# The state-space units of a hybrid decoder block, run in a staggered order of groups and chunks

## The chip, the core and the metric

The kernel runs on one core of one Trainium2 chip. The metric is the device time of one execution in microseconds (us); a smaller time is better. Three executions took 1394.72, 1395.9 and 1400.18 us, so the median is 1395.9 us.

## What is computed

One decoder block over 512 tokens of width 1024 in float32: a normalisation, one wide input projection, three token mixers in parallel (an attention with selected keys, an attention with compressed, selected and windowed keys, and a state-space mixer), gates that merge the three, an output projection, and a feed-forward part. The change touches the order of work in the state-space mixer, which the reference writes as

```python
cb = jnp.einsum('bcign,bcjgn->bcijg', cm, bm)
y_diag = jnp.einsum('bcijg,bcijgh,bcjgh,bcjghp->bcighp', cb, lmat, dtc, xs)
states = jnp.einsum('bcjgn,bcjgh,bcjghp->bcghpn', bm, decay_states * dtc, xs)
def step(h, inp):
    s_c, d_c = inp
    return h * d_c[..., None, None] + s_c, h
_, h_in = lax.scan(step, h0, (jnp.moveaxis(states, 1, 0), jnp.moveaxis(chunk_decay, 1, 0)))
y_off = jnp.einsum('bcign,bcghpn,bcigh->bcighp', cm, h_in, jnp.exp(a_cum))
y = y_diag + y_off + xs * d_skip.reshape(SSD_GROUPS, SSD_HPG)[:, :, None]
```

There are 4 groups (g) of 8 heads and 4 chunks (c) of 128 tokens. Chunk c of a group needs the state that chunk c-1 of the same group leaves behind; different groups do not depend on each other.

## The kernel before

Two generators write the program. `main` holds the latency-bound work: the index of the first attention, its units, then `ssd`, then the units of the second attention. `filler` holds the large projections: in this order z0 to z3, x0 to x3 (the inputs of the state-space groups 0 to 3), nq (the queries of the second attention), the merge gates, the branch products. `main` yields an amount of time after each piece, and the loop at the end lets `filler` emit that much; where `main` yields a name, such as `x2`, `filler` runs on until that part is emitted. The instructions of `main` get a higher priority (`HI`, `HM`), and the scheduler of the framework then lays out each engine's order, so that projection matmuls fill the places where `main` waits. PE, ACT, DVE and POOL each work through their own order, and SP issues nearly all DMAs in its order.

`ssd` runs 16 units, one for each (group, chunk). A unit goes through three parts.

- `stage1` takes a tile `bcx` (three matrices of the chunk) and a tile `E`, and has SP load both (L1248, L1250). `load_xz` loads `xz`, the inputs and the gate values (L1257). `xz` has two buffers, `bcx` and `E` have three.
- `stage2`: a small matmul (L1264), POOL masks `E` (L1265), ACT takes eight exponentials (L1268), POOL scales `xz` into `xt` (L1270), into `xw` where there is a next chunk (L1273), and by the skip weights (L1277). DVE multiplies `E` (L1275).
- `stage3`: where there is a chunk before, PE multiplies its state `hst` (L1286), DVE and POOL finish that (L1288, L1289). Where there is a chunk after, PE makes the new state (L1293), and ACT copies it (L1296) or POOL and DVE add it to the old one (L1298, L1299). Eight matmuls of `xt` with `E` follow (L1303, two passes each), DVE adds and gates the result (L1307, L1308), and ACT squares it into the gate half of `xz` (L1309). After that square the buffer of `xz` is free, and `load_xz` of the unit after the next is emitted. Four transposes (L1314) and a store end the unit one step later.

The list `order` sets which (group, chunk) is the unit number 0 to 15; `need(i)` yields `x` and `z` of a group before its chunk 0. Projection matmuls stand on L451 to L453, the transposes of the x projection on L835, those of nq on L601, the splitting of weights on L170 and L172, the convolution of x on L821 to L828.

Of the kernel before, what the change touches and what calls it, by code (L numbers as in the profile page):

```python
# [40 lines left out]
def build_kernel(ctx, tc, A, out):  # L41
# [1195 lines left out]
    def ssd(sv, ratio):  # L1237
# [82 lines left out]
            yield ratio * 100  # L1320

        TR = []
        order = [(g + i, c) for g in (0, 2) for c in range(4) for i in range(2)]

        def need(i):
            if i < 16:
# [341 lines left out]
    def main():  # L1668
        nonlocal at
        HI[0] = 0  # L1670
        yield from dsa_index(mk)
        yield "dq"
        yield "nkv"
        sv, *rest = yield from ssd_prelude()
        at = popen("att", side="right")
        HI[0] = HM
        us = dsa_units()
        us[5].load = lambda: ssd_prelude2(sv, *rest)
        us[7].load = lambda: ssd_prelude3(sv, rest[0])
        yield from pipeline(us, R1)  # L1680
        pclose("att")
        pclose("pre")
        pclose("mask")
        yield from ssd(sv, R3)
        XT[0] = "pT"
        yield "nq"
        at = popen("att", side="right")
        yield from pipeline(nsa_units(R2), R2)
        done.add("nsa")
        yield "c1"  # L1690
        pclose("att")
        pclose("kv")
# [60 lines left out]
```

## Time and profile before

| what | value |
|---|---|
| median of three executions | 1395.9 us |
| lowest and highest | 1394.72 and 1400.18 us |
| the profiled execution's own time | 1403.27 us |
| its span, first to last instruction | 1401.5 us |
| mean granted clock of TensorE, as a share of full speed | 0.986 |

The profile is one execution, about 7 us above the median. Its sums are made against its own span. A row of a timeline has a start, a duration, the engine, the line, the operation and its tiles, and in brackets the idle time of the engine before it with what ended that. `PEld` is the load of a matmul's weights, which overlaps `PE`.

### The profile page before, as it was taken

The page shows a single profiled execution, that of the slowest core. Times are in us where ns is not written, and L with a number is a line of the kernel's source. Part 1 is how long each engine was busy: PE and PEld are TensorE (multiplying, and loading weights), DVE is VectorE, ACT ScalarE, POOL GpSimd, SP SyncE. Part 2 cuts the span into 40 slices and gives each one's busy share as a digit, 9 for nine tenths or more (in the row PEclk, how much of TensorE's full clock was granted, in tenths as well). Part 3 has the DMA queues.
Part 4 walks back from the last instruction along what each step waited for, and adds up shares of the span by engine and source line. Part 5 has one row for each costly group of instructions (what it writes and reads, how often), then busy time and mean ns, then how long its engine had stood idle before and what let it go on. Part 6 is the DMA issues. An engine that isn't in the chain of part 4 may idle for free.

```text
span 1401.5 us, 19674 instructions
## 1 busy us (share of the span) xinstructions
PE 1369.0 (98%) x6875; PEld 1142.1 (81%) x6875; DVE 1001.1 (71%) x1962; ACT 722.0 (52%) x1434; POOL 286.8 (20%) x235
## 2 busy tenths in 40 slices
PE   8989999999999999999999999999899999999998
PEld 7878888888877778888887888788789888888887
DVE  6499977999877656477667788888635575767841
ACT  5545436667666756366565566555224444444430
POOL 3445211111047375100000002133100201102000
PEclk9999999999999999999999999999999999999999
DMA  6335654644486687735435453435444665746531
GB/s 192 89 96 144 166 179 132 166 113 123 121 259 223 190 257 201 188 100 140 114 114 157 118 146 111 122 117 177 143 150 140 118 177 127 174 116 132 157 117 52
DMA packets 222721, 205.35 MB, mean 147 GB/s; under 512 B 15497, under 2 KB 170013, under 8 KB 222622
## 3 DMA queue, kind: packets, MB, share of 16 engines
q1 hardware_dynamic: 206652, 180.49, 43.7%
q0 software_dynamic: 15232, 20.98, 8.2%
q10 hardware_dynamic: 738, 2.63, 0.6%
q8 instruction: 54, 0.88, 0.3%
q14 instruction: 45, 0.37, 0.1%
HBM read 167.56 MB, written 36.51 MB: 146 GB/s over the span
## 4 chain that ended last, share of the span: by engine, by line
PE 77%; DVE 7%; DMA 7%; issue 4%; POOL 3%; ACT 2%; SPq 0%; DVEq 0%; POOLq 0%; ACTq 0%
PE pj L451 18%; PE pj L453 18%; PE pj L452 18%; PE sc L451 3%; PE sc L452 3%; PE sc L453 3%; DMA gld<-g_d 3%; PE pT L931 2%; PE sc L893 2%; PE sc L892 2%; PE pv L944 2%; DMA wraw<-in_w_in_dram 1%; PE pv L943 1%; POOL mixf L1488 1%; PE sc L1303 1%
## 5 line engine op out<-in xcount | busy, mean ns | idle before, releaser
L170 ACT ACTIVATE whi<-wraw 128x1024 fp32r<-128x1024 f32 (+2 forms) x190 | 198.3, 1048 | 233.8 <-PE pj L452 115.7
L172 DVE TENSOR_TENSOR wlo<-wraw,whi 128x1024 fp32r<-128x1024 f32 (+1 forms) x169 | 215.7, 1280 | 104.5 <-ACT whi L170 102.9
L451 PE MATMUL pj<-hTh,whi 128*128 128x512 f32 x384 | 153.6, 400 | 0.2 <-DVE cacc L824 0.2
L453 PE MATMUL pj<-hTh,wlo 128*128 128x512 f32 x384 | 152.6, 397 | 0.0
L452 PE MATMUL pj<-hTl,whi 128*128 128x512 f32 x384 | 152.3, 397 | 0.0
L451 PE MATMUL pj<-whi,hTh 128*128 128x512 f32 (+2 forms) x352 | 138.7, 394 | 5.9 <-DVE stk L521 3.2
L901 ACT ACTIVATE p<-p,nb,rs 128x256 f32<-128x256 f32 (+3 forms) x192 | 123.2, 645 | 30.6 <-DVE nb L899 30.6
L453 PE MATMUL pj<-whi,hTl 128*128 128x512 f32 (+2 forms) x352 | 137.8, 392 | 0.1
L452 PE MATMUL pj<-wlo,hTh 128*128 128x512 f32 (+2 forms) x352 | 137.6, 391 | 0.0
L451 PE MATMUL pj<-yh,whi 128*128 128x512 f32 (+1 forms) x288 | 109.7, 387 | 11.0 <-DVE gld L1485 6.4
L452 PE MATMUL pj<-yl,whi 128*128 128x512 f32 (+1 forms) x288 | 109.2, 379 | 0.0
L453 PE MATMUL pj<-yh,wlo 128*128 128x512 f32 (+1 forms) x288 | 108.9, 378 | 0.0
L452 PE MATMUL pj<-h2l,whi 128*128 128x512 f32 (+1 forms) x256 | 96.3, 376 | 0.0
L453 PE MATMUL pj<-h2h,wlo 128*128 128x512 f32 (+1 forms) x256 | 96.2, 376 | 0.0
L451 PE MATMUL pj<-h2h,whi 128*128 128x512 f32 (+1 forms) x256 | 96.1, 376 | 0.0
L987 POOL DMA_DIRECT2D qu<-q_d x32 | 23.5, 735 | 334.9 <-PE sc L893 259.3
L451 PEld LDWEIGHTS pj<-hTh,whi 128*128 128x128 f32 x384 | 72.4, 189 | 14.0 <-DVE cacc L824 0.4
L452 PEld LDWEIGHTS pj<-hTl,whi 128*128 128x128 f32 x384 | 72.4, 189 | 13.8 <-issue 0.5
L453 PEld LDWEIGHTS pj<-hTh,wlo 128*128 128x128 f32 x384 | 72.4, 189 | 13.8 <-issue 0.2
L451 PEld LDWEIGHTS pj<-whi,hTh 128*128 128x128 f32 x352 | 67.4, 192 | 19.8 <-issue 5.8
L935 ACT ACTIVATE pth<-pT 128x512 fp32r<-128x512 f32 x95 | 54.5, 592 | 47.4 <-PE pT L931 46.9
L453 PEld LDWEIGHTS pj<-whi,hTl 128*128 128x128 f32 x352 | 67.4, 191 | 12.4 <-DVE hTl L427 0.4
(385 smaller groups left out, 3294.9 us busy)
## 6 DMA issues: line engine op xcount, KB each, us to landing
wraw<-in_w_in_dram SPq DMA_DIRECT2D x84, 512.0 KB, 4.7
wraw<-in_w_ff_dram SPq DMA_DIRECT2D x58, 512.0 KB, 4.3
qd<-in_w_ff_dram POOLq DMA_DIRECT2D x18, 512.0 KB, 6.0
q_d<-qev SPq DMA_DIRECT2D x64, 128.0 KB, 2.5
qu<-q_d POOLq DMA_DIRECT2D x32, 256.0 KB, 3.7
E<-ac_d SPq DMA_DIRECT2D x16, 512.0 KB, 4.9
xz<-xz_d SPq DMA_DIRECT2D x16, 512.0 KB, 5.8
gld<-g_d SPq DMA_DIRECT2D x32, 256.0 KB, 2.8
```

What stands on the lines that cost most here:

```text
L170: act.activation(hi[:, :m], r[:, :m], AF.Copy)
L172: (pool if i in LOWP else dve).tensor_tensor(lo[:, :m], r[:, :m], f(hi[:, :m]), op=ALU.subtract)
L451: pe.matmul(o, lh, rh, start=first, stop=False)
L452: pe.matmul(o, lh, rl, start=False, stop=False)
L453: pe.matmul(o, ll, rh, start=False, stop=last)
L892: pe.matmul(s_[:, h % w, :n], u.q[h], kh[:, :n], start=True, stop=False)
L893: pe.matmul(s_[:, h % w, :n], u.q[h], kl[:, :n], start=False, stop=True)
L901: act.activation(u.p[h][:, :n], u.p[h][:, :n], AF.Exp, bias=u.nb[:, h:h + 1], scale=rs8[:, u.b, u.h0 + h:u.h0 + h + 1], accum_out=u.sm[:, ...
L931: pe.transpose(pt[:, h], u.p[h][:, kb * 128:kb * 128 + 128], ident)
L935: act.activation(ph, ptf, AF.Copy)
L944: pe.matmul(o, vk, pl0, start=False, stop=en)
L987: pool.dma_start(q.rearrange("p (i a) c -> p i (a c)", i=2), src)
```

## The change

The list `order` is written out. Before, two groups alternate through all four chunks: (0,0) (1,0) (0,1) (1,1) and so on to (1,3), then the same with groups 2 and 3. Now group 0 runs its first two chunks, and each later group joins in one or two places behind: its first unit stands between units of the group before. Number, size and content of the units are the same.

```diff
-        order = [(g + i, c) for g in (0, 2) for c in range(4) for i in range(2)]
+        order = [(0, 0), (0, 1), (1, 0), (0, 2), (1, 1), (0, 3), (1, 2), (2, 0), (1, 3), (2, 1), (3, 0), (2, 2), (3, 1), (2, 3), (3, 2), (3, 3)]
```

In what follows u0 to u15 are the places in `order`. The orders below are those of PE and POOL; a line of three dots stands for projection matmuls (L451 to L453).

PE from the end of u0's matmuls to the first of u2, before (u1 is (1,0), u2 is (0,1); `xt` is the scaled input, `hst` a state, `craw` the x projection after its convolution):

```order
L1303 MATMUL sc<-xt,E 128x64 x6
L835 MATMUL pF<-ident,craw 128x128 x4
...
L1264 MATMUL pv<-bcx 128x128
L1303 MATMUL sc<-xt,E 128x64 x5
L1314 MATMUL pT<-ident,yv 128x128
L1293 MATMUL pT<-xw,bcx 128x512
L1314 MATMUL pT<-ident,yv 128x128 x3
L1303 MATMUL sc<-xt,E 128x64 x3
L1286 MATMUL sc<-hst,bcx 128x512
...
L1303 MATMUL sc<-xt,E 128x64 x3
```

The same stretch of PE now (u1 is (0,1), u2 is (1,0)):

```order
L1303 MATMUL sc<-xt,E 128x64 x6
L835 MATMUL pF<-ident,craw 128x128 x4
L1286 MATMUL sc<-hst,bcx 128x512
...
L1264 MATMUL pv<-bcx 128x128
...
L1303 MATMUL sc<-xt,E 128x64 x3
L1314 MATMUL pT<-ident,yv 128x128 x4
L1293 MATMUL pT<-xw,bcx 128x512
L1303 MATMUL sc<-xt,E 128x64 x5
...
L1303 MATMUL sc<-xt,E 128x64 x8
```

The product with the state moves ahead, since u1 now needs u0's state, and u2's matmuls stand behind 24 projection matmuls where there were 33.

PE around the last transposes of the x projection, before (the first L1303 row is u8, the last is u9, group 3's first unit):

```order
L1303 MATMUL sc<-xt,E 128x64 x5
L1264 MATMUL pv<-bcx 128x128
L835 MATMUL pF<-ident,craw 128x128 x4
...
L835 MATMUL pF<-ident,craw 128x128 x4
...
L1264 MATMUL pv<-bcx 128x128
L1314 MATMUL pT<-ident,yv 128x128 x4
...
L601 MATMUL pF<-ident,qraw 128x128 x4
...
L1303 MATMUL sc<-xt,E 128x64 x3
```

PE there now, from the end of u7 to the start of u9, which is (2,1); u10 is group 3's first unit:

```order
L1303 MATMUL sc<-xt,E 128x64 x5
L1264 MATMUL pv<-bcx 128x128
L1286 MATMUL sc<-hst,bcx 128x512
L835 MATMUL pF<-ident,craw 128x128 x4
...
L1303 MATMUL sc<-xt,E 128x64 x5
L1314 MATMUL pT<-ident,yv 128x128 x4
L1303 MATMUL sc<-xt,E 128x64 x3
L1286 MATMUL sc<-hst,bcx 128x512
L1264 MATMUL pv<-bcx 128x128
L835 MATMUL pF<-ident,craw 128x128 x4
...
L1303 MATMUL sc<-xt,E 128x64 x3
```

Before, the last four transposes were followed by 47 projection matmuls and nothing of u9; now they are followed by 13 and then by u9, which does not need group 3.

POOL, the piece of the difference at u2 and u3 (`E` is the decay matrix that POOL masks):

```order
 L1265 AFFINE_SELECT E<-E 128x1024
 L1277 TENSOR_TENSOR xz<-xz,dskip 128x512
+L1298 TENSOR_TENSOR hst<-hst,sv_dec 128x512
+L1289 TENSOR_TENSOR t_4105<-t_4105,xz 128x512
 L1265 AFFINE_SELECT E<-E 128x1024
-L1298 TENSOR_TENSOR hst<-hst,sv_dec 128x512
+L1270 TENSOR_TENSOR xt<-xz,sv_dth 128x512
+L1273 TENSOR_TENSOR xw<-xz,sv_dw 128x512
+L1277 TENSOR_TENSOR xz<-xz,dskip 128x512
+L1265 AFFINE_SELECT E<-E 128x1024 x2
 L1270 TENSOR_TENSOR xt<-xz,sv_dth 128x512
```

The masks of two later units (`x2`) now stand ahead of the scaling of u3's `xz`.

## Rows read from the trace of the kernel before

**Rows 1.** The page: the span, and each engine's busy time, share of the span and instructions.
```profile
span 1401.5 us, 19674 instructions
PE 1369.0 (98%) x6875; PEld 1142.1 (81%) x6875; DVE 1001.1 (71%) x1962; ACT 722.0 (52%) x1434; POOL 286.8 (20%) x235
```

**Rows 2.** Waits of PE, whole span: who waited for whom; us in total, times, longest.
```profile
PE sc L1303 <- POOL xt L1270: 6.3, 4, 2.2
PE pT L1293 <- POOL xw L1273: 0.7, 1, 0.7
PE pj L451 <- ACT yh L807: 4.6, 2, 2.7
PE pj L451 <- DVE gld L1485: 6.4, 8, 1.9
```

**Rows 3.** Where the projection stands: first and last of its steps, and unit 0's first load.
```profile
351.54 0.76 ACT L821 ACTIVATE cacc<-pj,convc 128x512 f32<-128x512 f32 x1
L835 PE MATMUL pF<-ident,craw x80: 270/272/300, 273.0 to 482.6; 128*128 128x128 f32 x80
390.61 0.38 SPq L1248 DMA_DIRECT2D bcx<-bct_d  x1
```

**Rows 4.** Chain of waits, 396 to 444: start us, us, what; two starts of projection matmuls included.
```profile
...
397.06 0.24 PE pj L451
...
401.16 0.23 PE pj L451
401.38 0.86 PE pT L1293 x2
...
403.09 0.28 PE pv L1264 x2
403.37 1.29 PE sc L1303 x12
404.66 0.44 PE pF L835 x4
...
442.20 0.91 PE sc L1286 x2
...
```

**Rows 5.** From unit 0's gate to unit 2's scale: timelines of ACT, SP and POOL.
```profile
410.60 0.62 ACT L1309 ACTIVATE xz<-yv 128x512 f32<-128x512 f32 x1
411.34 0.36 SPq L1257 DMA_DIRECT2D xz<-xz_d  x1
417.57 1.04 POOL L1270 TENSOR_TENSOR xt<-xz,sv_dth 128x512 f32<-128x512 f32 x1 [5.34 <-DMA xz<-xz_d]
```

**Rows 6.** Timeline of PE: the four stalls on xt; idle time before in brackets.
```profile
418.67 0.88 PE L1303 MATMUL sc<-xt,E 128*128 128x64 f32 x6 [1.18 <-POOL xt L1270]
438.79 0.88 PE L1303 MATMUL sc<-xt,E 128*128 128x64 f32 x6 [1.16 <-POOL xt L1270]
463.76 1.44 PE L1303 MATMUL sc<-xt,E 128*128 128x64 f32 x10 [1.77 <-POOL xt L1270]
496.92 0.88 PE L1303 MATMUL sc<-xt,E 128*128 128x64 f32 x6 [2.18 <-POOL xt L1270]
```

**Rows 7.** Busy time by stretch: us, each engine's busy time, granted clock, DMA share, GB/s.
```profile
418.00:426.00 8.00, 6.68 (x29) 4.57 (x30) 5.23 (x6) 2.77 (x9) 8.00 (x8) 0.79 0.79 256
436.00:444.00 8.00, 6.84 (x38) 4.96 (x37) 3.88 (x7) 5.11 (x18) 6.22 (x6) 1.00 0.88 304
462.00:470.00 8.00, 6.24 (x32) 5.77 (x33) 7.00 (x10) 5.77 (x20) 4.57 (x5) 0.79 0.89 278
496.00:504.00 8.00, 6.96 (x29) 5.14 (x30) 1.94 (x3) 1.49 (x3) 8.00 (x9) 0.79 0.45 119
505.00:565.00 60.00, 60.00 (x329) 48.71 (x328) 37.94 (x50) 39.20 (x100) 40.47 (x28) 1.00 0.84 239
750.00:775.00 25.00, 22.82 (x106) 19.34 (x107) 15.84 (x46) 14.68 (x34) 1.43 (x2) 0.86 0.51 143
```

**Rows 8.** The tile xz: POOL's scaling of it, ns min/median/max of one.
```profile
L1270 POOL TENSOR_TENSOR xt<-xz,sv_dth x16: 1033/1042/2085, 398.4 to 549.5; 128x512 f32<-128x512 f32 x16
```

## The prediction

> **What bounds the kernel now.** I read the page first. Its table of engines has PE busy 1369.0 of 1401.5 us [rows 1], so an order of units can win only what PE does not do: idle time, and matmuls that run at the lower clock. The instructions stay the same, 6664 matmuls by the orders of both kernels, so the question is where PE waits. PE's waits name three late groups [rows 2]: the state-space products wait for the scaled input `xt` (6.3 us in 4 stalls, 0.7 more for `xw` behind the first), the branch products wait for their split inputs (4.6 us) and for gate tiles (6.4 us). Only the first group lies in the stage that the change reorders.
>
> The timeline of PE places the four stalls: 1.18 us at 418.7, 1.16 at 438.8, 1.77 at 463.8 and 2.18 at 496.9 [rows 6]. The table of stretches shows what three of them cost besides. The 8 us around the first, the third and the fourth have a mean granted clock of 0.79, so part of each ran at 1.2 instead of 2.4 GHz; around the second it stayed at 1.00 [rows 7]. A loss of 0.21 of 8 us is 1.68 us each time. The stage therefore loses 6.3 + 0.7 = 7.0 us of idle time and 3 x 1.68 = 5.0 us of clock, 12.0 us in all. From 505 to 565 us PE is busy for all 60.00 us at full clock [rows 7], so the last units wait for nothing.
>
> Why is `xt` late? `xz` has two buffers, so the load for one unit starts after the square of the unit two places before. For u0 and u2 the square starts at 410.60, SP issues at 411.34, POOL scales at 417.57 [rows 5] and PE starts at 418.67 [rows 6], though u0's last matmul of this kind was done at 404.66 (where the next row of the chain starts [rows 4]). **That is a chain of 14.0 us** against which PE needs other work. The fourth stall has another cause: u9 is group 3's first unit, and the last transposes of the x projection start at 482.6 [rows 3], 14.3 us before u9's matmuls.
>
> **The change, part by part.** *Removed, added:* nothing; every unit does the same work, and SP and POOL issue the same loads and operations.
>
> *The start.* Group 0's first two units no longer need group 1's inputs. This wins nothing: the convolution of group 1's last step starts at 351.54, and unit 0's first load is issued at 390.61 [rows 3], because the first attention ends only then. PE's order is the same down to the transposes behind u0.
>
> *The places of the matmuls.* I price PE's work between the last L1303 of a unit and the first of the unit two places on, by rows 4: a projection matmul 0.228 us (18 of them from 397.06 to 401.16), L1293 0.86, L1286 0.91, L1264 0.28, four transposes 0.44, eight L1303 1.7 (16 passes at 1.29/12). From u0 to u2 before: 33 projection matmuls (7.5), two sets of x transposes (0.9), two L1264 (0.6), u1's eight L1303 (1.7), L1314 (0.4), L1293 (0.9), L1286 (0.9), together 12.9 us; with the stall of 1.2 the chain took 14.1. Now it is 24 projection matmuls and otherwise the same work, 10.9 us. The same count for the later places:
>
> before, u3 to u11: 13.1, 11.7, 14.5, 13.0, 11.8, 12.9, 27.1, 25.7, 11.7 us;
> now, u3 to u15: 11.8, 16.7, 14.9, 12.5, 14.0, 16.3, 11.5, 13.4, 13.9, 13.4, 13.6, 18.8, 19.3 us.
>
> Before, u4 stalled with 11.7 (chain 12.9), u7 with 11.8 (chain 13.6), u2 with 12.9 (14.1), and u6 with 13.0 did not stall. So while the x projection runs a chain takes 12.9 to 14.1 us, and what is short of that is a stall. Now:
>
> - **u2:** engines and queues are the same up to there, so the same 14.1: 14.1 - 10.9 = 3.2 us. Ends 2.0 (chain 12.9) and 4.3 (chain 14.1 and one more POOL operation of 1.04, as in the next paragraph).
> - u3 has 11.8 us, but u2's stall lies within it, 15.0. POOL's order has the mask of u5 ahead of u3's scaling, and its load waits for u2's matmuls. From u2's end to u3's start PE has 8.4 us; a load like that of rows 5 (6.2) and two POOL operations (2 x 1.04 [rows 8]) are 8.3, so it fits: 0.
> - **u6:** 12.5 against 13.0, which sufficed: 0.5. Ends 0 and 1.6.
> - **u9**, now (2,1): 11.5 against 13.3, the middle of u4's and u7's chains: 1.8. Ends 1.4 and 2.6.
> - **u10**, group 3's first unit: 11.8 us of work after the last transposes, with u9's 1.8 and the clock's 1.7 it is 15.3, over the 14.3 that it took before [rows 3, 6]: 0. The stall of 2.18 goes; what is late next is u9.
> - u11 to u15 have 13.4 or more, in the stretch where 11.7 was enough: 0.
>
> Idle: 3.2 + 0.5 + 1.8 = 5.5 us. Two of these are as long as those that lowered the clock: 2 x 1.68 = 3.4 (ends one and three times). Together 8.9 against 12.0 us: **3.1 us less**. The low ends give 2.0 + 0 + 1.4 + 1.7 = 5.1 (6.9 less), the high ends 4.3 + 1.6 + 2.6 + 5.0 = 13.5 (1.5 more).
>
> A row and a rule of the Trainium skill on POOL: its scaling takes 1.04 us in the middle and 2.09 at most [rows 8], twice as long. The skill's page SBUF — State Buffer, section "SBUF: two separate sides", says that VectorE operations with two SBUF inputs and GpSimd operations share a port pair by "an exclusive lock, not a bandwidth split", so that one blocks for the whole of the other. By that rule a denser run of units would lengthen these chains, and the stage would lose instead of win; the trace agrees as far as the doubled operation goes. The third rival works it out from rows.
>
> *Behind the stage.* The second attention's first matmul now stands after 1702 projection matmuls instead of 1733, 7.1 us earlier; its last product with values stands after 2866 instead of 2856. PE has the same matmuls before and behind, so this alone is worth 0; its cover is that projections remain to fill the second attention's waits, and 1958 of 4824 still follow its end.
>
> The profiled span becomes 1401.5 - 3.1 = 1398.4 us, its own time 1403.27 - 3.1 = 1400.2. That execution lies 7.4 us above the median of 1395.9, which becomes **1392.8 us**.
>
> **The rivals.**
> *No effect (1395.9):* nothing waits for a group's first unit but u9, and the stalls only trade places. For it: three of the four stalls have the `xz` chain, which the change leaves as it is.
> *All stalls go (1395.9 - 12.0 = 1383.9):* the chain shrinks to 10.9 us, since the units are mixed, some with no old state, some with no new one, and POOL has less to do at once. For it: after 505 us a place of 11.7 us sufficed. Against it: there the convolutions are over, which fill DVE and ACT before.
> *Slower, a longer chain:* one POOL operation of each chain takes 2.09 instead of 1.04, so 14.1 becomes 15.1 at every place. Stalls, each counted into the place behind it: u2 4.2, u5 0.2, u6 2.4, u9 3.6, u11 1.2, u12 0.5, u13 1.0, together 13.1, and four long ones cost 6.7 of clock: 19.8 against 12.0, so 1395.9 + 7.8 = 1403.7. It decides from a chain of about 15 us in all places. For it: two masks now stand ahead of one scaling. Against it: the longest chain seen is 14.1.
> *The branch products:* the second attention's units fall on other projection matmuls. Their waits for split inputs are 4.6 us [rows 2], and the 25 us from 750 lose 0.14 x 25 = 3.5 to the clock [rows 7]. Without both it is 1392.8 - 8.1 = 1384.7, with twice as much 1400.9.
>
> **How the numbers follow.** My forecast has 0.50, no effect 0.12, all stalls gone 0.19, the longer chain 0.13, the branch products 0.06, half each way. About 0.5%, 7.0 us, is what a measurement of this kernel can tell from no change, so the bounds are 1388.9 and 1402.9. Faster: 0.19 + 0.03 = 0.22. Slower: 0.13. Within: 0.50 + 0.12 + 0.03 = 0.65. The forecast's own ends are 1389.0 and 1397.4. The range reaches from 1385 to 1402: it leaves out about half of the fast case and most of the slow one, 2 in 10.
>
> **What would show it.** In the profile of the changed kernel PE should wait for `xt` at u2 for about 3 us near 415 to 419, again near u9, and not at group 3's first unit; two stretches of the stage, not three, should have a clock below 1.00. The second attention should start about 10 us earlier. I am wrong if PE's wait for `xt` sums to under 3 or over 9 us, or if the branch products' waits move by more than the stage does.

## The result and the profile after

The changed kernel takes 1410.06 us (median of 5 executions, 1407.66 to 1413.52), the kernel before beside it 1395.9 (5 executions). The ratio is 1.0098 with a 95% interval of 1.0079 to 1.0118: slower by 1%, some 14 us, where 1392.8 was forecast and 1402 was the upper end of the range.

The profiled execution took 1409.28 us, in the middle of its runs. The page's span and engines, answering to [rows 1]:

```profile
span 1407.6 us, 19671 instructions
PE 1366.0 (97%) x6875; PEld 1134.5 (81%) x6875; DVE 1002.9 (71%) x1962; ACT 722.9 (51%) x1434; POOL 289.9 (21%) x235
```

PE is busy for 3 us less than in [rows 1], in a span that is 6.1 us longer: what was added is waiting. PE's waits over the whole span, answering to [rows 2] (who waited for whom; us in total, times, longest):

```profile
PE pj L451 <- DVE gld L1485: 11.2, 10, 1.6
PE sc L1303 <- POOL xt L1270: 4.5, 4, 1.8
PE pj L451 <- ACT yh L807: 3.3, 3, 1.9
...
PE pT L1314 <- DVE yv L1308: 2.7, 3, 1.7
...
PE sc L1286 <- ACT hst L1296: 1.0, 1, 1.0
PE sc L1303 <- DVE yv L1307: 0.8, 1, 0.8
```

The wait for `xt` went from 6.3 to 4.5 us, as wanted (a second profile of the kernel before, e5, has 3.9). Two things stand against it. The stage waits for a state (`hst`) and longer for the gated result (`yv`); these waits were 0 and 0.2 us in the rows, and 0 and 1.8 in e5. And the branch products, 400 us behind the stage, wait 11.2 us for gate tiles instead of 6.4.

The stalls of PE in the stage, from its timeline (start, duration, engine, line, operation; in brackets the idle time and what ended it):

```profile
407.63 1.12 PE L1286 MATMUL sc<-hst,bcx 128*128 128x512 f32 x2 [1.03 <-ACT hst L1296]
...
420.21 2.04 PE L1303 MATMUL sc<-xt,E 128*128 128x64 f32 x16 [1.68 <-POOL xt L1270]
...
432.96 1.77 PE L1303 MATMUL sc<-xt,E 128*128 128x64 f32 x14 [0.71 <-POOL xt L1270]
...
452.88 0.88 PE L1303 MATMUL sc<-xt,E 128*128 128x64 f32 x6 [1.76 <-POOL xt L1270]
...
463.53 1.11 PE L1314 MATMUL pT<-ident,yv 128*128 128x128 f32 x4 [1.71 <-DVE yv L1308]
...
488.13 0.88 PE L1303 MATMUL sc<-xt,E 128*128 128x64 f32 x6 [0.34 <-POOL xt L1270]
```

The table of stretches at the places of [rows 7] (us, busy time of PE, PEld, DVE, ACT, POOL, granted clock, DMA share, GB/s):

```profile
418.00:426.00 8.00, 6.32 (x28) 4.43 (x27) 7.43 (x9) 4.66 (x12) 4.74 (x4) 0.79 0.75 241
436.00:444.00 8.00, 7.47 (x40) 5.83 (x38) 4.82 (x8) 0.73 (x3) 7.92 (x7) 1.00 0.73 227
462.00:470.00 8.00, 6.47 (x23) 4.79 (x24) 7.56 (x10) 5.48 (x17) 2.01 (x2) 0.79 0.86 251
496.00:504.00 8.00, 6.94 (x37) 4.94 (x36) 3.61 (x6) 5.00 (x15) 5.66 (x6) 1.00 0.60 195
505.00:565.00 60.00, 57.99 (x311) 46.59 (x310) 37.09 (x49) 37.39 (x91) 37.60 (x25) 1.00 0.75 218
```

Two stretches of the stage are at the lower clock, not three, and group 3's first unit (now at 497.8 us) no longer waits for `xt`. Both were forecast. But the 60 us from 505, in which PE did not wait at all before, now hold 2.0 us of waiting.

### The profile page after: what moved, and what is told of

Same layout as the page of the kernel before. It is cut to its first block, busy times and chain, and to the rows that moved or that the text cites. A ratio compares the mean times of both kernels' runs of the same rounds, so it can differ in the third digit from the quotient of the medians.

```text
span 1407.6 us, 19671 instructions
## 1 busy us (share of the span) xinstructions
PE 1366.0 (97%) x6875; PEld 1134.5 (81%) x6875; DVE 1002.9 (71%) x1962; ACT 722.9 (51%) x1434; POOL 289.9 (21%) x235
## 4 chain that ended last, share of the span: by engine, by line
PE 71%; DVE 9%; DMA 8%; issue 5%; POOL 4%; ACT 3%; SPq 1%; DVEq 0%; POOLq 0%; ACTq 0%
PE pj L451 16%; PE pj L453 16%; PE pj L452 16%; PE sc L453 3%; PE sc L452 3%; PE sc L451 3%; DMA gld<-g_d 3%; PE pT L931 2%; DMA E<-ac_d 2%; PE sc L893 2%; POOL mixf L1488 2%; DMA wraw<-in_w_in_dram 2%; PE sc L892 2%; PE pv L944 1%; PE pv L943 1%
## 5 line engine op out<-in xcount | busy, mean ns | idle before, releaser
L172 DVE TENSOR_TENSOR wlo<-wraw,whi 128x1024 fp32r<-128x1024 f32 (+1 forms) x169 | 212.3, 1261 | 93.2 <-ACT whi L170 91.6
L451 PE MATMUL pj<-hTh,whi 128*128 128x512 f32 x384 | 156.3, 407 | 0.2 <-DVE cacc L824 0.2
L453 PE MATMUL pj<-hTh,wlo 128*128 128x512 f32 x384 | 152.7, 398 | 0.0
L451 PE MATMUL pj<-whi,hTh 128*128 128x512 f32 (+2 forms) x352 | 139.6, 396 | 5.7 <-DVE stk L521 3.2
L453 PE MATMUL pj<-whi,hTl 128*128 128x512 f32 (+2 forms) x352 | 138.1, 393 | 0.0
L451 PE MATMUL pj<-yh,whi 128*128 128x512 f32 (+1 forms) x288 | 107.9, 380 | 14.6 <-DVE gld L1485 11.2
L453 PE MATMUL pj<-yh,wlo 128*128 128x512 f32 (+1 forms) x288 | 106.8, 371 | 0.0
L453 PE MATMUL pj<-h2h,wlo 128*128 128x512 f32 (+1 forms) x256 | 96.2, 376 | 0.0
L451 PE MATMUL pj<-h2h,whi 128*128 128x512 f32 (+1 forms) x256 | 96.1, 376 | 0.0
L452 PEld LDWEIGHTS pj<-hTl,whi 128*128 128x128 f32 x384 | 72.7, 189 | 15.3 <-issue 1.8
L451 PEld LDWEIGHTS pj<-hTh,whi 128*128 128x128 f32 x384 | 72.7, 189 | 15.2 <-issue 1.7
L453 PEld LDWEIGHTS pj<-hTh,wlo 128*128 128x128 f32 x384 | 72.4, 188 | 14.1 <-issue 0.2
L451 PEld LDWEIGHTS pj<-whi,hTh 128*128 128x128 f32 x352 | 67.7, 192 | 19.6 <-issue 5.5
L452 PEld LDWEIGHTS pj<-wlo,hTh 128*128 128x128 f32 x352 | 67.6, 192 | 13.8 <-DVE wlo L172 1.1
```

The source lines that it names most:

```text
L172: (pool if i in LOWP else dve).tensor_tensor(lo[:, :m], r[:, :m], f(hi[:, :m]), op=ALU.subtract)
L451: pe.matmul(o, lh, rh, start=first, stop=False)
L452: pe.matmul(o, lh, rl, start=False, stop=False)
L453: pe.matmul(o, ll, rh, start=False, stop=last)
```

## The experiments

The theories at first: (1) the stage itself loses the 14 us; (2) the loss arises behind the stage, because the second attention starts 31 projection matmuls earlier against the projections; (3) any other order upsets the layout by chance. Every ratio is to the kernel before, run beside them on the same chip. Its medians were 1395.6 us beside e1 to e4, 1395.0 beside e5 to e8, 1395.9 beside e9 to e12 and 1393.9 beside e13 to e16, so a difference between runs of two of these groups is good to about 2 us.

### e1, e2: one half of the new order

```diff
+ e1: order = [(0,0),(0,1),(1,0),(0,2),(1,1),(0,3),(1,2),(1,3)] + [(g, c) for c in range(4) for g in (2, 3)]
+ e2: order = [(g, c) for c in range(4) for g in (0, 1)] + [(2,0),(2,1),(3,0),(2,2),(3,1),(2,3),(3,2),(3,3)]
```

> Only groups 0 and 1 are staggered; groups 2 and 3 alternate as before. By the built order the second attention's first matmul stands after 1734 projection matmuls, as before (1733; 1702 with the whole change). Theory 1, the loss of 14 us arises in the state-space stage itself (the wait of u1 for u0's state, 1.03 us at 407.6, and the short waits for yv): this half carries most of those waits, so 1402 to 1408 us. Theory 2, the loss arises behind the stage, because the second attention starts some 30 projection matmuls earlier against the projections and its end then meets the branch products otherwise: the start is the old one here, so 1394 to 1400 us. Theory 3, any other order upsets the schedule by chance: no value is favoured, and its sign need not follow the start of the second attention.

> Only groups 2 and 3 are staggered; groups 0 and 1 alternate as before. The second attention's first matmul stands after 1699 projection matmuls (1733 before, 1702 with the whole change). Theory 1 (loss inside the stage): the first half's waits are those of before, so 1396 to 1402 us. Theory 2 (loss behind the stage, by the early start of the second attention): nearly all of the loss is here, 1405 to 1412 us, and the wait of the branch products for the gate tiles is above 9 us (6.4 before, 11.2 with the whole change). Theory 3: no value favoured.

e1 took 1402.3 us, ratio 1.0048 (1.0031 to 1.0064); e2 1399.9, ratio 1.0033 (1.0020 to 1.0045). Each half costs something, 6.7 and 4.3 us, and neither alone is the change. e1 is slower though its second attention starts at the old place, so theory 2 alone is wrong; e2 is slower though its first half is the old one. Its waits for gate tiles are 7.7 us, where theory 2 expected more than 9.

### e3, e4: the branch products' gates mended, in both kernels

The branch products run in the order a0, c0, c1, b0, b1, b2: a is the first attention, b the second and c the state-space mixer; b1 and b2 take the second half of b's inputs, each for one half of the tokens. `gld` is a gate tile that multiplies a product, `yh` a split input, `mixf` the sum to which the gated product is added.

```diff
+                if br in COLS:
+                    g2 = g_.rearrange("p (k q) -> p k q", k=2)
+                    nc.sync.dma_start(g2, g_d[(bi * 8 + m) * 128:(bi * 8 + m + 2) * 128, c0:c1].rearrange("(k p) q -> p k q", p=128))
+                    th_[n], th_[n + 1] = g2[:, 0], g2[:, 1]
+                    return
...
+                if br in COLS and m % 2 == 0:
+                    load_g(8 * bi + m + 2)
...
-                (dve if br in ("b1", "b2") else pool).tensor_tensor(mx, mx, th, op=ALU.add)
+                (dve if br in ("b0", "b1", "b2") else pool).tensor_tensor(mx, mx, th, op=ALU.add)
```

> The kernel before, with the branch products' gates mended: for b1 and b2, whose gate tiles are half as wide, one load brings two of them into one buffer, so that four gates are ahead instead of two, and b0's last add runs on DVE instead of POOL. Most of the 6.4 us of PE's waits for gate tiles should go, and with them the stretch at the lower clock near 1011 to 1018 us (some 3 us). All theories: 1388 to 1394 us; if the waits move to something else, 1395 to 1398.

> The same mending of the gates in the changed kernel. Here the waits for gate tiles are 11.2 us. Theory 1 (the loss lies in the stage): the distance to the mended kernel before stays near 14 us, so about 1402 to 1407 us. Theory 2 (the loss lies in the branch products): the distance shrinks to 3 to 7 us, what the stage itself lost in the traces (idle time between 400 and 600 us rose by 3.0 us), so 1392 to 1400 us. Theory 3: the distance may be anything, also below zero.

e3 took 1389.6 us, ratio 0.9946 (0.9930 to 0.9961); e4 1397.9, ratio 1.0009 (0.9999 to 1.0020). The edit is worth 6.0 us in the kernel before and 12.1 in the changed one, so the distance falls from 14.2 to 8.3 us. That lies between what theories 1 and 2 expected. The edit takes 6 us more out of the changed kernel, but where it does so is not shown: by the reckoning by parts below, b1 and b2 lose 2.2 us in e3 and 3.2 in e4 (7.7 and 9.9 without the edit), so the distance falls by 1.2 us there, and c1 and b0 still lose 5.5 and 9.6 (5.6 and 10.2).

### e5: the kernel before, once more

> The kernel before, unchanged, profiled once more, since its profiled execution (1403.27 us, granted clock 0.986) stood 7 us above its median. All theories: 1393 to 1398 us with a mean clock near 0.99, and 5 to 8 us less lost to the lower clock after 400 us than in that execution; so the stretches at 752 to 758, 902 to 905 and 1011 to 1018 us should mostly be gone. If they are all there again, they belong to the kernel and the change removed them.

e5 took 1395.6 us at the median (ratio 1.0008, 0.9995 to 1.0020), and its profiled execution 1393.5, span 1391.8. The stretches at 750 and 900 us, 0.86 in [rows 7] for the first, are at full clock here:

```profile
432.00:440.00 8.00, 8.00 (x34) 5.72 (x33) 6.79 (x9) 6.34 (x21) 4.79 (x6) 0.83 0.91 303
494.00:502.00 8.00, 7.22 (x30) 4.99 (x31) 2.18 (x3) 1.73 (x3) 8.00 (x9) 0.79 0.55 164
505.00:565.00 60.00, 60.00 (x327) 48.49 (x326) 36.64 (x48) 37.47 (x97) 38.08 (x27) 1.00 0.83 237
750.00:775.00 25.00, 25.00 (x134) 21.03 (x133) 19.52 (x54) 17.48 (x41) 1.43 (x2) 1.00 0.63 177
900.00:925.00 25.00, 25.00 (x133) 21.02 (x132) 22.96 (x60) 16.95 (x40) 6.96 (x4) 1.00 0.45 138
```

Of the stage's three low stretches of [rows 7] only the last is at its place; 418 to 426 and 462 to 470 are at 1.00, but another lies at 432 (0.83). So the stage has two here and not three, and the stretches behind 600 us, on which a rival of the prediction drew, belonged to that one execution. PE's waits in the stage are the measure for what follows (400 to 600 us):

```profile
PE sc L1303 <- POOL xt L1270: 3.9, 3, 2.2
PE pT L1314 <- DVE yv L1308: 1.8, 1, 1.8
PE pT L1293 <- POOL xw L1273: 1.3, 2, 0.7
```

That is 7.0 us. The changed kernel has 4.5 + 2.7 + 1.0 + 0.8, and three more of 0.5 to 0.6: 10.7 us.

### e6: the second attention held back in the changed order

```diff
+MGW = 2
...
+            if m == MGW:
+                dve.scalar_tensor_tensor(kc[:, 0, 0, 0:1], th[:, 0:1], 0.0, f(kc[:, 0, 0, 0:1]), op0=ALU.mult, op1=ALU.add)
+                done.add("mgw")
...
         yield "nq"
+        yield "mgw"
+        yield -20000.0
```

(`th` is a merge gate, `kc` a constant of the second attention's first products. The negative amount gives back to `main` what the projections ran ahead. So the edit moves the second attention's start, and its pace against the projections behind the start as well.)

> The changed order, and the second attention held back: its first product reads a constant through one small VectorE operation that waits for the third merge gate (31 projection matmuls later; the value is unchanged). By the built order its first matmul then stands after 1734 projection matmuls, as before, its last product with values after 2880 (2856 before, 2868 with the change alone). Theory 2 (the early start costs): 1399 to 1404 us, the waits for gate tiles fall back to some 7 us. Theory 1 and a third theory (the loss is made of the stage's own waits and of how the last units of the second attention meet b0): no gain, 1408 to 1414 us, since the end comes still later.

e6 took 1394.7 us, ratio 0.9994 (0.9983 to 1.0006). **One small operation that makes the second attention start later takes back all of the loss**, some 15 us, with the changed order of units left in place; either theory expected less of it (1399 us at best). PE's waits behind 600 us, of e5:

```profile
PE pj L451 <- DVE gld L1485: 7.2, 8, 1.8
PE pj L451 <- ACT yh L807: 2.3, 2, 1.6
```

and of e6, whose lines stand one to four further down:

```profile
PE pj L452 <- DVE gld L1489: 6.6, 8, 1.6
PE pj L452 <- ACT yh L811: 0.5, 1, 0.5
```

against 11.2 and 3.3 in the changed kernel.

### e7, e8: three buffers for xz, in both kernels

```diff
-            xz = sp.tile([128, 2, 512], F32, name="xz", bufs=2)
+            xz = sp.tile([128, 2, 512], F32, name="xz", bufs=3)
...
-                hn = sp.tile([128, 512], F32, name="hst", bufs=4)
+                hn = sp.tile([128, 512], F32, name="hst", bufs=3)
...
-                ev = sp.tile([128, 4, 128], F32, name="yev", bufs=2)
+                ev = sp.tile([128, 4, 128], F32, name="yev", bufs=1)
```

> The kernel before with three buffers for xz instead of two, so that a unit's load no longer waits for the square of the unit two places before; to make room hst has three buffers instead of four and yev one instead of two. PE's waits for xt (6.3 us) should fall under 2.5 us, with one or two of the stretches at the lower clock (1.7 us each). All theories: 1388 to 1393 us; 1395 or more if the waits move to E or to the loads of bcx.

> The same three buffers in the changed order (xt waits 4.5 us there). Theory 1 (the loss lies in the stage's waits on the chain through xz): the distance to the kernel before with three buffers shrinks below 6 us, 1390 to 1398 us. Theory 2 (the loss lies behind the stage): the second attention starts after 1702 projection matmuls as in the changed kernel, so the distance stays 9 us or more, 1400 to 1406 us.

e7 took 1390.2 us, ratio 0.9963 (0.9950 to 0.9977); e8 1404.0, ratio 1.0062 (1.0047 to 1.0076). The third buffer (with one buffer fewer for `hst` and `yev`) is worth 5 to 6 us in either, and the distance stays at 13.8. Theory 1 in this form falls: the loss is not on the chain through `xz` that the prediction priced.

### e9: the order before, held back in the same way

> The order before with the same small operation that holds the second attention back. It holds nothing much here: the first product stands after 1734 projection matmuls instead of 1733, but from there on PE's order is that of e6, product for product. The two kernels differ in the state-space stage alone. Theory 2 (the start of the second attention decides): the stage by itself costs the changed order little, so 1389 to 1394 us, 1 to 5 below e6 (1394.7). Theory 4 (the operation itself, or the projections emitted around it, give the gain of e6, whatever the order): the 15 us are gained here too, 1380 to 1385. Theory 1 (the stage costs the changed order its 14 us, and e6 gained them elsewhere): about 1381 as well, 14 below e6.

e9 took 1390.3 us, ratio 0.9964 (0.9949 to 0.9980). Theory 4 falls, since the operation gains 5.6 us here and 15.3 in e6. From the second attention on the orders of PE in e9 and e6 are the same, so the 4.4 us between them are put down to the stage (by parts below, 3.1 us of them show there).

### e10, e14: other places for the start

The edit is that of e6 with another gate: `MGW = 1` in e10, `MGW = 3` in e14.

> The changed order, held back by the gate before that one: the second attention's first product stands after 1710 projection matmuls (1702 without the hold, 1734 in e6), its last product with values after 2916 (2868, 2880). Theory 2 in its plain form (every matmul by which it starts early costs alike, 14 us for 31): 1405 to 1410 us. Theory 3 (no rule in the start; how the units happen to meet the branch products decides): anything between 1392 and 1412, and a value under 1400 would speak for it, since only 8 matmuls separate this kernel from the changed one.

> The changed order, held back by the gate after that of e6: the second attention starts after 1758 projection matmuls, its last product with values after 2964 (2880 in e6), twelve matmuls ahead of the end of b1's (2976). If later is better: 1388 to 1393 us. If the meeting with the branch products decides: b1 and b2 now wait for the last units, 1396 to 1406 us, with their cost in the stages b1 and b2.

e10 took 1400.0 us, ratio 1.0027 (1.0012 to 1.0043); e14 1393.1, ratio 0.9991 (0.9977 to 1.0004). With starts after 1702, 1710, 1734 and 1758 projection matmuls the changed order takes 1410.1, 1400.0, 1394.7 and 1393.1 us. Later is better, but most is gained by the first 8 matmuls, and the last 24 give less than the spread of the runs. Theory 2 in its plain form (every matmul alike, 1405 to 1410 us for e10) falls. e10 differs from the change by more than 8 matmuls at the start: behind it fewer of the second attention's products are done at nearly every point, 373 against 396 at the end of the merge gates. The loss that e14 was expected to have in b1 and b2 did not come.

### e11, e12, e13: u1 and u2 exchanged

```diff
- [(0, 0), (0, 1), (1, 0), (0, 2), (1, 1), ...
+ [(0, 0), (1, 0), (0, 1), (0, 2), (1, 1), ...
```

e11 is the change with this edit, e12 is e1 with it, e13 is e11 held back as in e6.

> The changed order with u1 and u2 exchanged: (0,0) (1,0) (0,1) and then as in the change. u1 is another group's first unit again, so that nothing waits for u0's state (1.03 us) and the chains of the first units are those of before. The second attention starts after 1702 projection matmuls, and PE's order behind is that of the changed kernel. Theory 2: the stage gains 1 to 4 us, all else stays, 1405 to 1409 us. Theory 1 (the dense start of group 0 is the loss): 1396 to 1402 us.

> As e1 (groups 0 and 1 staggered, 2 and 3 as before; 1402.3 us), with u1 and u2 exchanged as in e11. From the second attention on PE's order is that of the kernel before, product for product, so what it differs by from before is the stage alone. If e1's loss of 6.7 us came from the start of group 0 (state wait, two units of one group in succession): 1394 to 1398 us. If a staggered order costs the stage by itself, wherever it starts: 1400 to 1404 us. Theory 2 has to lie near 1396 (1393 to 1399).

> The changed order with u1 and u2 exchanged (e11) and the second attention held back (e6). From there on PE's order is that of e6 and e9. If the two causes add up and nothing else of the change costs: as e9 (1390.3), 1388 to 1392 us. If the rest of the staggered order costs something that e11 did not show: 1393 to 1398. If e6 and e11 removed the same loss twice over: 1394 to 1396, as e6.

e11 took 1402.4 us, ratio 1.0050 (1.0031 to 1.0069); e12 1395.8, ratio 0.9999 (0.9985 to 1.0013); e13 1389.6, ratio 0.9968 (0.9953 to 0.9983). The exchange is worth 7.7 us (against the change; 6.7 by the two ratios), 6.5 (against e1) and 5.2 (against e6; 3.6 by the two ratios). With the change and e6 PE's order from the second attention on is the same with the exchange and without it, so there the gain is put down to the stage; with e1 it is not the same (134 and 154 products in the table's last column). e11's 1402.4 us lie between what its two theories expected. In e12 it takes back the whole loss of e1, and in e13, where both causes are undone, nothing of the change's loss is left against e9. PE's waits of e11 in the stage, 400 to 600 us:

```profile
PE pv L1264 <- DMA bcx<-bct_d: 2.7, 1, 2.7
PE sc L1303 <- POOL xt L1270: 1.7, 2, 0.9
PE pv L1264 <- DVE t L1288: 1.6, 1, 1.6
PE pT L1293 <- POOL xw L1273: 1.2, 2, 0.7
```

They sum to 7.2 us, about as in e5, with `xt` at 1.7: the rest of the staggered order does shorten the waits for `xt`, and pays for it with a load of `bcx` and with PE's wait behind L1288.

### e15, e16: the version that beats both

The edits of e3, e6 and e7 together, on the order before (e15) and on that of e11 (e16).

> The order before with everything that gained: the second attention held back (e9: 5.6 us), three buffers for xz (e7: 4.8 us), the gates of b1 and b2 in pairs and b0's adds on DVE (e3: 6.0 us). If the three add up: 1379 to 1382 us. If the gates' mending and the held start remove the same waits: 1383 to 1387.

> The same three edits on the changed order with u1 and u2 exchanged. If an order of units is worth nothing once the waits for xz are gone: within 2 us of e15. If the staggered order has a gain of its own there (group 3's first unit no longer waits for its transposes): 2 to 5 us below e15.

e15 took 1382.9 us, ratio 0.9918 (0.9896 to 0.9940), 11 us below before; e16 1388.5, ratio 0.9959 (0.9946 to 0.9973). The three edits add up only in part: alone they gained 5.6, 4.8 and 6.0 us, 16.4 in sum, together 11.0. The time lies between the two cases, next to the second (1383 to 1387), in which the gates' mending and the held start remove the same waits. The order of units has no gain of its own there; e16's order is the slower one by 5.6 us, which neither case expected.

## Where the time went, part by part

The profiles can be compared by parts of the projections, which every kernel works through in the same sequence of 4824 matmuls. For each product of PE I take the time from its start to the next product's start, less the median of that time for products of the same kind over all eighteen profiles. The sum over a part is what PE lost there, idle time, clock and small gaps in one. Parts: up to matmul 1290; the state-space stage to 1632; the merge gates to 2208; the branches a0 and c0, c1 and b0, b1 and b2; the rest loses 0.3 to 1.1 us in all of these. The last column counts the second attention's products that PE runs among those of c1.

| kernel (start of the second attention) | median us | before the stage | stage | gates | a0, c0 | c1, b0 | b1, b2 | beside c1 |
|---|---|---|---|---|---|---|---|---|
| before, the execution of the rows (1733) | 1395.9 | 22.4 | 14.1 | 4.2 | 8.2 | 6.6 | 8.7 | 154 |
| e5, before (1733) | 1395.6 | 21.5 | 12.8 | 4.4 | 3.4 | 5.6 | 7.7 | 154 |
| the change (1702) | 1410.1 | 23.8 | 17.9 | 3.8 | 5.5 | 10.2 | 9.9 | 122 |
| e1, first half (1734) | 1402.3 | 22.5 | 18.3 | 4.5 | 3.9 | 7.7 | 10.0 | 134 |
| e2, second half (1699) | 1399.9 | 20.4 | 14.8 | 3.1 | 4.2 | 10.0 | 8.3 | 130 |
| e3, before, gates mended (1733) | 1389.6 | 22.2 | 13.2 | 4.6 | 4.4 | 5.5 | 2.2 | 154 |
| e4, the change, gates mended (1702) | 1397.9 | 22.6 | 15.7 | 3.8 | 5.3 | 9.6 | 3.2 | 122 |
| e12, e1 exchanged (1733) | 1395.8 | 24.5 | 12.1 | 4.8 | 4.7 | 5.8 | 8.8 | 154 |
| e11, exchanged (1702) | 1402.4 | 21.9 | 12.5 | 3.8 | 5.9 | 11.2 | 9.0 | 122 |
| e10, held (1710) | 1400.0 | 21.2 | 16.3 | 3.0 | 6.6 | 8.5 | 7.3 | 131 |
| e6, held (1734) | 1394.7 | 22.5 | 15.5 | 2.8 | 2.9 | 4.3 | 7.3 | 168 |
| e14, held (1758) | 1393.1 | 20.9 | 14.5 | 2.7 | 5.4 | 3.3 | 4.0 | 182 |
| e9, before, held (1734) | 1390.3 | 22.2 | 12.4 | 3.7 | 3.1 | 3.6 | 6.1 | 168 |
| e13, exchanged, held (1734) | 1389.6 | 19.6 | 11.6 | 2.8 | 2.7 | 3.1 | 6.2 | 168 |

From e5 to the change the sum grows by 15.8 us, as the span does: 2.3 ahead of the stage, where the kernels are the same and single executions differ by up to 5; **5.1 in the stage; 8.4 behind it, 4.6 of them in c1 and b0**.

*The stage.* Where u1 is (0,1) the column says 14.5 to 18.3, where it is (1,0) 11.6 to 14.8, whatever follows. One pair of profiles is not its price: the four of the order before (the rows, e3, e5, e9) have 13.1 in the mean, the five of the changed order (the change, e4, e6, e10, e14) 16.0, so 2.9 us by the means against 5.1 by the pair. What is new starts at u0. PE, DVE and ACT of the changed kernel around u0's end (timeline; the first row comes right behind u0's last L1303):

```profile
405.99 0.61 PE L835 MATMUL pF<-ident,craw 128*128 128x128 f32 x4
```

```profile
407.19 1.22 DVE L1275 TENSOR_TENSOR E<-E,pv 128x1024 f32<-128x1024 f32 x1 [1.29 <-ACT E L1268]
...
410.04 0.68 DVE L1307 TENSOR_TENSOR yv<-sc,xz 128x512 f32<-128x512 f32 x1
410.64 0.68 DVE L1288 TENSOR_TENSOR t<-sc,sv_ea 128x512 f32<-128x512 f32 x1
411.23 1.33 DVE L1308 TENSOR_TENSOR yv<-yv,xz 128x512 f32<-128x512 f32 x1
```

```profile
407.00 0.57 ACT L1296 ACTIVATE hst<-pT 128x512 f32<-128x512 f32 x1
...
413.09 0.62 ACT L1309 ACTIVATE xz<-yv 128x512 f32<-128x512 f32 x1
```

The first and the last of these in e5:

```profile
403.56 0.61 PE L835 MATMUL pF<-ident,craw 128*128 128x128 f32 x4
```

```profile
409.98 0.61 ACT L1309 ACTIVATE xz<-yv 128x512 f32<-128x512 f32 x1
```

u1 needs the state that ACT has only just copied (PE's 1.03 us at 407.63). And because u1 now has an old state, its step L1288 stands on DVE between u0's add and u0's gate; before, u1 had no such step. u0's square, which frees the buffer of `xz` for u2, comes 7.1 us after the end of u0's matmuls; in e5 it is 6.4, in the rows 5.9 (404.66 [rows 4] to 410.60 [rows 5]). But u2's matmuls start 14.2 us after that end now (420.21), 14.2 in e5 (417.81) and 14.0 in the rows, so the later square did not lengthen the chain to u2. What u2 loses more (1.68 against 0.93 and 1.18) comes with PE's shorter work, as predicted, and the state's 1.03 us come on top.

Further on a chain does get longer. In the 8 us from 436 POOL is busy for 7.92 us, against 6.22 in [rows 7], and DVE waits for it before u3's result:

```profile
439.62 0.69 DVE L1307 TENSOR_TENSOR yv<-sc,t 128x512 f32<-128x512 f32 x1 [3.18 <-POOL t L1289]
```

u3's square then starts at 445.47, and u5, which was given no stall, stalls for 1.76 us; its chain from the end of u3's matmuls (435.19) to 452.88 is 17.7 us long. That the places of u1 and u2 decide is shown by e11 and e13. Which of the later waits hang on them, beyond the 1.03 us for the state, is not shown.

*Behind the stage.* The stage now ends with fewer projection matmuls done (its last L1303 stands after 1605 of them, before after 1644), so more of the second attention's products are run early, beside the merge gates: 396 of its 896 there, against 370 before and 352 in e6. They are then missing where the branch products wait for their split inputs and gates. In the table the loss of c1 and b0 goes with the last column: 122 products go with 9.6 to 11.2 us, 130 to 134 with 7.7 to 10.0, 154 with 5.5 to 6.6, 168 with 3.1 to 4.3, 182 with 3.3. That the second attention's place against the projections decides is shown by e6, e9, e10 and e14, which move its start and its pace and leave the order of units; that the missing products are what makes it cost is read from the table, and no run changed their number alone.

POOL's adds stand in the chain of waits there. The chain of the changed kernel at the end of b0 (start, us, what):

```profile
978.28 2.55 POOL mixf L1488
980.85 3.83 DMA gld<-g_d
984.81 0.70 DVE gld L1485
985.58 3.45 POOL mixf L1488 x2
...
991.39 2.21 POOL mixf L1488
...
994.51 3.58 DMA gld<-g_d
```

The adds L1488 took 1278, 1296 and 2553 ns (lowest, median, highest) in e5, and in the changed kernel:

```profile
L1488 POOL TENSOR_TENSOR mixf<-mixf,gld x24: 1278/1488/3385, 839.8 to 991.4; 128x512 f32<-128x512 f32 x24
```

By the Trainium skill, page SBUF — State Buffer, section "SBUF: two separate sides", VectorE operations with two SBUF inputs and GpSimd operations that read SBUF block each other for a whole instruction. The longer adds agree with it: the longest, 3.38 us from 885.97 in the changed kernel, has DVE's L172 with the inputs `wraw` and `whi` (1.20 us at 886.41) and two L808 with `yr` and `yh` within its time. That they cost anything here is not shown: e4, which moves b0's adds to DVE, also loads the gates in pairs, so it doesn't part the two, and c1 and b0 still lose 9.6 us there.

## Why the prediction was wrong, by its steps

- **The start wins nothing:** right. The state-space stage (its first L1264) begins at 397.0 us, against 395.5 before.
- **u2, 3.2 us (2.0 to 4.3):** right in kind. The stall for `xt` is 1.68 us, and 1.03 more were spent on u1's state just ahead, 2.7 together. The chain from u0's last matmul (about 406) to 420.21 is some 14.2 us, where 14.1 was taken. The stall is shorter than 3.2 because PE spent more ahead of it, 1.03 us of it waiting.
- **u3 and u5 at 0, u6 0.5, u9 1.8:** u3 lost 0.71 and u5 1.76, u6 nothing on `xt`, u9 0.34. The sum for `xt` was 4.5 against 5.5, but by other units, so that it came near is luck. The reckoning took a chain of 12.9 to 14.1 us for every place; u5's was 17.7.
- **u10, group 3's first unit, 0, and two stretches at the lower clock:** right, but e5 has two as well, so the third that the sum took off was no gain of the order.
- **"u11 to u15 have 13.4 or more ...: 0":** wrong, 2.0 us between 505 and 565.
- **The sum of the stage, 3.1 us less:** wrong, it became 5.1 more between the two traces (2.9 by the means of nine) and 4.4 (e6 against e9) to 7.7 (the change against e11) between runs. The step that failed is the one that counted only stalls on `xt`: "Now it is 24 projection matmuls and otherwise the same work". The work is the same for PE, but u1 now depends on u0. Its wait for the state (1.03 us), the waits for `yv` (2.7 and 0.8; 1.8 in e5) and the longer chain of u5 have no term. In the prediction's own terms the stage has 10.7 us of waits and two low stretches of 1.7, 14.1 us, where 8.9 was forecast. The 12.0 us set against it were also too much: 7.0 of waits and two low stretches are 10.4 in e5.
- **"Behind the stage ... this alone is worth 0":** wrong, and the largest error. It argued that PE has the same matmuls ahead and behind, and that enough projections remain to cover the second attention. It left out that the second attention covers the projections too, those of the branches, whose inputs and gates come late. Differences between runs put the price at 6.6 (e11 against e12: the starts of 1702 and 1733) to 9.7 us (the 15.3 us that the hold gives in the change, less the 5.6 that it gives in the order before). The start itself was forecast about 10 us earlier; it came at 574.0 against 576.7 us, 2.7 earlier, since the stage lost time. The last product with values stands after 2868 projection matmuls, not 2866.
- **The rivals:** the chain longer by a doubled POOL scaling did not occur; all sixteen scalings L1270 took 1033 to 1049 ns. Where a chain did grow, at u5, POOL's other operations stood in it, and not in all places. The rival that came true in kind was the branch products, at 0.06 and half of that on the slow side: their waits for split inputs and gates are 14.5 us, against 11.0 in [rows 2] and 9.5 in e5. Its terms did not come true. The waits for split inputs, which it doubled, fell from 4.6 to 3.3 us, and the clock at 750 us, which it doubled too, is at 1.00; what rose were the waits for gate tiles, which it did not price. That its 1400.9 is near to what the start alone costs (e11: 1402.4) is luck, and the stage's own loss came on top. The text had named a sign of being wrong, branch waits that move by more than the stage does: against e5 they did (5.0 us against 3.7 of waits in the stage), against the execution of the rows they moved alike (3.5 and 3.5).

Still open: why the staggered order with u1 and u2 exchanged loses 5.6 us to the old one once `xz` has three buffers (e16 and e15). By the same reckoning 5.1 of it lie in the stage (16.2 against 11.1 us); the 200 us from 400 have a granted clock of 0.97 and 0.98, so part of it is the clock, and PE waits 1.7 us for `xt` in e16 and not at all in e15.

## What to carry to other kernels

A stage that fills the gaps of a long filler is itself the filler of something later: when a reordered stage lets the next latency-bound part start earlier, ask which late waits lose their cover, and try a hold of that start before giving up the order. When units are reordered, follow each unit's dependences on the one right ahead (here one state), on all engines and not on the bottleneck's order alone. And take a second profile of the same kernel before pricing clock losses: what two executions of it don't share can't be put down to the order of its work.

## What had not been expected

The same kernel, profiled twice, spent 1401.5 and 1391.8 us. The two differ in stretches at the lower clock: the first has 0.79 around 418 and 462 us and 0.86 from 750 [rows 7], the second 1.00 at all three, with stalls of similar size (1.18 us at 418.67 [rows 6], 0.93 at the same place in e5); the second has a stretch of its own at 432, which the first has not. A start of the second attention that is later by 8 projection matmuls, 1.8 us of work, went with 10.0 us (the change and e10), though the hold moves the pace behind the start too.
